# Gated delta rule in a hybrid layer: 32x32 diagonal blocks inverted by substitution on GpSimd, gates and key products moved ahead of the query and value convolutions

## The chip, the cores and the metric

The program runs on one core of a Trainium2 chip. The metric is device time in microseconds (us); several runs of a kernel are compared by their median. The engines are TensorE (PE; its weight loads are listed as PEld), VectorE (DVE), ScalarE (ACT), GpSimd (POOL) and SyncE (SP), which here issues nearly all DMAs.

## The reference, cut to what matters

One step of a hybrid layer, all in float32, for 512 prompt tokens and 64 sample tokens, with a model width of 1024. In the order of the computation: RMS norm and one input projection; a short convolution with SiLU over q, k and v; the gated delta rule with 4 heads of 128; differential attention; output projection; attention over a memory of 256 rows; a feed-forward block of 4096; a last norm. The change lies in the gated delta rule:

```
G    = cumsum(g)                                # per chunk of tokens
gam  = where(tril, exp(G[i] - G[j]), 0)
a    = where(strict, beta[i] * (k k^T) * gam, 0) + I
u, w = triangular_solve(a, [beta * v, beta * exp(G) * k])     # unit lower triangular
qk   = (q k^T) * gam
# scan over the chunks with the state S:
vn = u - w S;  o = (q exp(G)) S + qk vn;  S = S exp(G_last) + (k exp(G_last - G))^T vn
```

The norms of q and k are divided out along the way. The kernel takes chunks of 128 tokens (four of the prompt) and one of 64 (the sample), so that there are 18 heads-times-chunks groups of 32 rows: 4 chunks of 4 blocks and one of 2, each for 4 heads, 72 blocks of 32 by 32 in all.

## The kernel before, in words

Weights come in blocks of 128 columns by `weights`: a DMA into one of three buffers `raw`, a cast to `wh` on ACT (L164), the remainder `wl` on DVE (L165). `project` multiplies a block with the normed tokens on PE (L110), in a half of 256 tokens and one of 320, into three PSUM banks `pr`; a callback empties each bank (for the half of 256 a copy on ACT and an addition on DVE, L197 and L198). A scheduler fixes the order of the instructions on each engine when the program is built; an engine then works through its own list and waits on semaphores, so whatever stands behind a waiting instruction waits too.

Stages in order: 12 convolution blocks, k first, then q, then v (L407 to L427); the gates (L429 to L504), whose matmul takes the columns `wab`; the norm of the memory rows (L517 to L529); level masks `lev` (L533 to L549); for each chunk `gdn_prep`; the z projection, 4 blocks (`project_z`); `gdn_scan` for each chunk, beside which the projections of the differential attention run; the attention itself; and from `pr<-wh,u` on the keys and values of the memory and the rest of the layer.

`gdn_prep` builds the strict upper triangular `At` of a chunk for 4 heads (L617), and inverts I+At by doubling: from blocks of 1 (X and its transpose Dt) to 2, 4, 8, 16, 32 and 64. Each level takes a masked copy `B` of At on DVE (L642), a product with Dt and a copy `Y` on ACT (L664), a product with X, a subtraction from Dt on DVE (L669), and a transposition of Dt, copied to X on ACT (L673). The banks `g0` (even chunks) and `g1` (odd chunks) hold these products; `gs` holds those of the scan. `rpow` (L211) takes a power on GpSimd.

Of the kernel before, what the change touches and what calls it, by code (L numbers as in the profile page):

```python
# [34 lines left out]
def hybrid_layer_kernel(  # L35
# [373 lines left out]
    for typ in (1, 0, 2):
        cT[typ] = (e5[:, 1], e2[:, 1], e2[:, 0])[typ]  # L410
        for h in range(H):
            m = typ * 4 + h
            if m in FIRST:
                project(wts[m], xs, ev[m], halves=HALVES[1:])
            else:
                project(weights(w2, m * P), xs, conv_input(m))
            cb = cbs[m]
            G.tensor_copy(cb[:, SOFF : SOFF + 3], cwt[:, m, 4:7])
            n = SOFF + DEC
            yv = small("yv", [P, 584])  # L420
            A.activation(yv[:, :n], cb[:, :n], AF.Identity, scale=cwt[:, m, 0:1])  # L421
            for i in range(1, 4):
                V.scalar_tensor_tensor(yv[:, :n], cb[:, i : i + n], cwt[:, m, i : i + 1], yv[:, :n], ALU.mult, ALU.add)  # L423
            A.activation(cT[typ][:, h, :SEQ], yv[:, :SEQ], AF.Silu)
            A.activation(cT[typ][:, h, SEQ:], yv[:, SOFF:n], AF.Silu)
            G.tensor_copy(cst[:, m, 0:3], cb[:, SEQ : SEQ + 3])
            G.tensor_copy(cst[:, m, 3:6], cb[:, SOFF + DEC : SOFF + DEC + 3])  # L427

        if typ == 1:  # L429
            with tc.issue_after(opened[mybir.EngineType.PE]), tc.issue_after(opened[mybir.EngineType.Activation]):  # L430
                for q in range(2):
                    for t in range(0 if q else 2, 5):
                        raw_out(t, q, turn(xt[t], TT[t][1], q, f"g{t % 2}"))
            for i in range(2):
                nc.sync.dma_start(hd[i], hst[i])

# [68 lines left out]


# [8 lines left out]


    mt = view(e3, 0, 2, D)  # L517
    tc.keep_in_program_order(nc.sync.dma_start(mt, mem_prompt[0].rearrange("(b p) d -> p b d", p=P)))
    gkv = gain_rows(ln_mem_kv[0], "qz1")
    mn = view(e5, 0, 2, D)  # L520
    mhl = pair(4, F32R)
    mh, ml = view(mhl, 0, KT, NMEM), view(mhl, 1, KT, NMEM)
    for bi in range(2):
        scale(mn[:, bi, :], mt[:, bi, :], root(squares(mn[:, bi, :], mt[:, bi, :], P), P), gkv, P)
        for q in range(2):
            src = turn(mn[:, bi, :], P, q, "ba")
            mhi, mlo = (x[:, 4 * q : 4 * q + 4, bi * P : (bi + 1) * P] for x in (mh, ml))
            A.copy(mhi, src)
            V.tensor_tensor(mlo, src, mhi.bitcast(F32), ALU.subtract)  # L529


    with tc.issue_after(opened[mybir.EngineType.DVE]), tc.issue_after(opened[mybir.EngineType.Pool]):
        lev = const([P, P], "lev")  # L533
        prev = ident
        for lb in range(7):
            s = 2 << lb
            e = small("X", [P, P])
            G.memset(e, 1.0)
            ev = e.rearrange("p (n s) -> p n s", s=s)
            G.affine_select(out=ev, in_=ev, pattern=[[-s, P // s], [0, s]], compare_op=ALU.is_ge, fill=0.0, base=0, channel_multiplier=1)  # L540
            G.affine_select(out=ev, in_=ev, pattern=[[s, P // s], [0, s]], compare_op=ALU.is_ge, fill=0.0, base=s - 1, channel_multiplier=-1)
            m = small("B0", [P, P])
            V.tensor_tensor(m, e, prev, ALU.subtract)
            if lb == 0:
                V.tensor_copy(lev, m)
            else:
                V.scalar_tensor_tensor(lev, m, float(1 << lb), lev, ALU.mult, ALU.add)
            prev = e
        V.tensor_tensor(lev, lev, triu, ALU.mult)  # L549


    ck, cq, cv_ = cT[1], cT[0], cT[2]
    chunks = [(c, c * 128, c * 128, 128) for c in range(4)] + [(4, 512, 512, 64)]

    def v4(ap, n):
        return ap.rearrange("p (h n) -> p h n", h=4)[:, :, :n]

    def sb(tag, bufs=2):
        return small(tag, [P, 4, P], bufs)
# [654 lines left out]
```

## Time and profile before

| | |
|---|---|
| median of 3 runs | 1062.87 us (1062.4 to 1063.59) |
| span of the profiled execution | 1061.8 us |
| PE busy | 1037.3 us (98%) |
| DVE busy | 673.3 us (63%) |
| ACT busy | 433.7 us (41%) |
| POOL busy | 72.5 us (7%) |
| PE in the chain that ended last | 89% |

The profiled execution's own time is its span of 1061.8 us; the runs' median stands 1.1 us above it. The first matmul of the memory's keys, after which the change touches no order that matters for the delta rule, starts at 374.09 us. A reader looks first at the busy shares, then at the chain that ended last, then at the windows by stage, and at what PE waited for in the stage that changes.

### The profile page before, as it was taken

What the parts mean: (1) busy time and instruction counts of PE and PEld (TensorE: products, weight loads), DVE (VectorE), ACT (ScalarE), POOL (GpSimd) and SP (SyncE); (2) the same over time, 40 slices, a digit from 0 to 9 for tenths busy, and PEclk for the clock granted to TensorE, in tenths of its full rate; (3) what the DMA queues carried; (4) which work ended last, traced back from release to release, by engine and by line L of the source; (5) the groups of instructions that cost most, each with busy time, mean ns of one, the idle gap of its engine ahead of it and who ended that gap; (6) DMA issues with size and microseconds to landing.
All of it is one profiled execution on the core that took longest, in us unless ns stands there. A gap on an engine that the chain in (4) does not pass through costs nothing.

```text
span 1061.8 us, 16966 instructions
## 1 busy us (share of the span) xinstructions
PE 1037.3 (98%) x6574; PEld 933.5 (88%) x6574; DVE 673.3 (63%) x1487; ACT 433.7 (41%) x905; POOL 72.5 (7%) x126
## 2 busy tenths in 40 slices
PE   8999999999999999999999999999999999999997
PEld 6999889898788877999887799999999999999996
DVE  6766684766567575564554666666666666666774
ACT  6644754333265665343333443323232323222344
POOL 4311120221000000000000000000000000000000
PEclk9999999999999999999999999999999999999998
DMA  7332310100132255524111132232314141313312
GB/s 211 109 125 70 122 40 21 42 1 22 41 100 63 67 200 198 165 80 141 58 40 40 47 90 64 60 99 60 105 55 120 50 120 50 110 54 110 92 53 90
DMA packets 139443, 89.97 MB, mean 85 GB/s; under 512 B 5522, under 2 KB 130576, under 8 KB 138852
## 3 DMA queue, kind: packets, MB, share of 16 engines
q1 hardware_dynamic: 138996, 88.24, 27.9%
q8 instruction: 52, 0.85, 0.3%
q10 hardware_dynamic: 368, 0.66, 0.2%
q14 instruction: 27, 0.22, 0.1%
HBM read 79.14 MB, written 9.74 MB: 84 GB/s over the span
## 4 chain that ended last, share of the span: by engine, by line
PE 89%; issue 4%; DVE 3%; ACT 2%; POOL 1%; DMA 0%; POOLq 0%; ACTq 0%
PE pr L110 69%; PE g L110 9%; PE gs L110 3%; PE ba L116 3%; PE ba L110 2%; PE g L116 2%; POOL tg L211 1%; DVE B L642 0%; DMA out_dram<-p 0%; POOL tiny L211 0%; PE pr L116 0%; DVE wl L165 0%; DVE Dt L669 0%; PE gs L116 0%; ACT wh L164 0%
## 5 line engine op out<-in xcount | busy, mean ns | idle before, releaser
L110 PE MATMUL pr<-x,wh 128*128 128x512 f32 (+1 forms) x2664 | 700.2, 344 | 1.1 <-DVE u L953 0.6
L110 PEld LDWEIGHTS pr<-x,wh 128*128 128x128 f32 x2664 | 457.5, 189 | 36.9 <-issue 1.1
L110 PE MATMUL pr<-x,wl 128*128 128x256 f32 (+1 forms) x1776 | 486.3, 300 | 0.0
L110 PEld LDWEIGHTS pr<-x,wl 128*128 128x128 f32 x1776 | 329.4, 189 | 8.4 <-issue 0.4
L164 ACT CAST wh<-raw 128x1024 fp32r<-128x1024 f32 (+1 forms) x153 | 136.5, 892 | 232.8 <-PE pr L110 218.3
L165 DVE TENSOR_TENSOR wl<-raw,wh 128x1024 fp32r<-128x1024 f32 (+1 forms) x153 | 157.4, 1029 | 61.9 <-ACT wh L164 60.2
L953 DVE TENSOR_TENSOR u<-u,pr 128x256 f32<-128x256 f32 (+1 forms) x160 | 72.5, 453 | 63.4 <-PE pr L110 60.5
L211 POOL TENSOR_TENSOR tiny<-tiny,nhalf 128x1 f32<-128x1 f32 (+4 forms) x11 | 10.1, 916 | 665.8 <-DVE tiny L1144 409.2
L204 ACT CAST x<-p 128x256 fp32r<-128x256 f32 x64 | 27.8, 434 | 51.8 <-DVE p L1081 51.8
L110 PE MATMUL pr<-wh,u 128*128 128x512 f32 x128 | 41.4, 401 | 0.0
L205 DVE TENSOR_TENSOR x<-p,x 128x256 fp32r<-128x256 f32 x64 | 29.2, 457 | 15.1 <-ACT x L204 15.1
L197 ACT COPY p<-pr 128x256 f32<-128x256 f32 (+1 forms) x44 | 16.4, 373 | 51.5 <-PE pr L110 51.5
L198 DVE TENSOR_TENSOR p<-pr,p 128x256 f32<-128x256 f32 (+1 forms) x44 | 18.6, 423 | 26.6 <-ACT p L197 26.6
L955 DVE TENSOR_TENSOR u<-u,pr 128x256 f32<-128x256 f32 x80 | 33.6, 420 | 2.4
L1080 DVE TENSOR_TENSOR p<-pr,rB 128x320 f32<-128x320 f32 x32 | 15.7, 491 | 26.0 <-PE pr L110 26.0
L423 DVE SCALAR_TENSOR_TENSOR p<-p,gcol,p 128x579 f32<-128x579 f32 x33 | 27.1, 821 | 6.4 <-ACT p L421 5.9
L1081 DVE SCALAR_TENSOR_TENSOR p<-p 128x256 f32<-128x256 f32 x64 | 29.3, 458 | 2.2
L673 ACT COPY X<-g 128x512 f32<-128x512 f32 (+1 forms) x24 | 13.2, 550 | 42.6 <-PE g L116 42.5
L110 PE MATMUL g<-u,qz 128*128 128x256 f32 (+4 forms) x96 | 29.6, 409 | 0.1
L207 ACT ACTIVATE x<-u,gcol 128x256 fp32r<-128x256 f32 (+1 forms) x32 | 17.0, 534 | 30.7 <-DVE u L955 30.7
L642 DVE SCALAR_TENSOR_TENSOR B<-lev,At 128x512 f32<-128x512 f32 (+1 forms) x30 | 20.8, 697 | 10.6 <-PE g L110 8.8
L110 PEld LDWEIGHTS pr<-wh,u 128*128 128x128 f32 x128 | 23.3, 189 | 4.2
(319 smaller groups left out, 1217.7 us busy)
## 6 DMA issues: line engine op xcount, KB each, us to landing
raw<-in_w_ff_dram SPq DMA_DIRECT2D x32, 512.0 KB
raw<-in_w_ff_dram SPq DMA_DIRECT2D x64, 256.0 KB
raw<-in_w_in_dram SPq DMA_DIRECT2D x28, 512.0 KB
raw<-in_w_mem_k_dram SPq DMA_DIRECT2D x8, 512.0 KB
raw<-in_w_mem_v_dram SPq DMA_DIRECT2D x8, 512.0 KB
raw<-in_w_out_dram SPq DMA_DIRECT2D x8, 512.0 KB
raw<-in_w_mem_q_dram SPq DMA_DIRECT2D x8, 512.0 KB
raw<-in_w_mem_o_dram SPq DMA_DIRECT2D x8, 512.0 KB
```

The lines of the kernel that those rows point to most:

```text
L110: i = nc.tensor.matmul(out, lhsT, rhs, start=start, stop=stop)
L116: i = nc.tensor.transpose(out, in_, ident[:n, :n])
L164: A.copy(wh, raw)
L165: V.tensor_tensor(wl, raw, wh.bitcast(F32), ALU.subtract)
L204: A.copy(h, src)
L205: V.tensor_tensor(lo, src, h.bitcast(F32), ALU.subtract)
L211: G.tensor_tensor(out, in_, bc(nhalf[: in_.shape[0], 0:1], list(in_.shape)), ALU.pow)
L423: V.scalar_tensor_tensor(yv[:, :n], cb[:, i : i + n], cwt[:, m, i : i + 1], yv[:, :n], ALU.mult, ALU.add)
L642: V.scalar_tensor_tensor(B[:n, :, :n], lev[:n, :n].unsqueeze(1).to_broadcast([n, 4, n]), float(lv), At[:n, :, :n], ALU.is_equal, ALU.mult,)
L953: V.tensor_tensor(hm, hm, b, ALU.add)
L955: V.tensor_tensor(hm, hm, more, ALU.add)
L1081: V.scalar_tensor_tensor(f, f, 0.0, f, ALU.max, ALU.mult)
```

## The change

The doubling up to blocks of 32 goes. Of every `At` the 32x32 diagonal blocks of all chunks and heads are gathered, through DRAM (`dA`), on 72 partitions, one block to a partition, and inverted there together by forward substitution on GpSimd: 31 steps of a product (L586) and a subtraction (L590). The result goes through DRAM (`dD`) into the diagonal of each chunk's `Dt`; a transposition on DVE (L662) gives X, and the levels 32 and 64 follow as before.

For this the gates come after the first k block; `gr` holds the cumulated gates as rows, which go through DRAM (`dG`) and come back broadcast over the partitions (`g_rows`) in place of the matmul with `triu`. The decays `gam`, the products `k k^T` and `At` of all chunks are made once the k blocks are done, and then the q and v blocks follow. `gdn_prep` is parted into `gdn_products` and `gdn_inverse`; z is projected whole between the products of chunk 0 and its inverse. The norm of the memory rows moves behind the scans, with smaller loads; some buffers change places, and the memory's values are projected before its keys.

```diff
+    def conv_block(typ, h):
...
+    conv_block(1, 0)
...  (gates)
     mm(gsum[:, 0:20], triu, ggf)
     mm(gsum[:, 20:40], ones, ggf)
+    gr = bank()
+    mm(gr[:20, :P], ggf, triu)
+    grow_s = small("B1", [20, P])
+    A.copy(grow_s, gr[:20, :P])
+    nc.sync.dma_start(dG, grow_s)
...
+    for h in range(1, H):
+        conv_block(1, h)
...
+    def g_rows(c):
+        t = sb("B0" if c % 2 else "B1")
+        nc.sync.dma_start(t.rearrange("p h n -> p (h n)"), dG[4 * c : 4 * c + 4, :].rearrange("h i -> (h i)").partition_broadcast(P))
+        return t
...
+    for c, c0, t0, n in chunks:
+        g = g_rows(c)
+        for h in range(H):
+            V.scalar_tensor_tensor(
+                gam[c][:, h], g[:n, h, :n], Gc[:n, c, h : h + 1], cap[:n, :n], ALU.subtract, ALU.min
+            )
+    A.activation(gam4, gam4, AF.Exp)
+    A.activation(gam[4], gam[4], AF.Exp)
+    for c, c0, t0, n in chunks:
+        bkk = bank(f"g{c % 2}")
+        for h in range(H):
+            mm(bkk[:n, h * P : h * P + n], ck[:, h, L], ck[:, h, L])
+        dg = sb("Y" + str(c % 2))
+        V.tensor_tensor(dg[:n, :, :n], v4(bkk, n)[:n], ident[...], ALU.mult)
+        V.tensor_reduce(sk[:n, c, :], dg[:n, :, :n], AX.X, ALU.add)
...
+        for h in range(H):
+            V.scalar_tensor_tensor(
+                At[c][:, h], bkk[:n, h * P : h * P + n], brk[:n, c, h : h + 1], gam[c][:, h], ALU.mult, ALU.mult
+            )
+        nc.sync.dma_start(dA[c], At[c])
+        for b in range(n // BL):
+            nc.sync.dma_start(
+                AB[at : at + 4].rearrange("h (r i) -> h r i", r=BL), dA[c][bs, :, bs].rearrange("r h i -> h r i")
+            )
...
+    for j in range(BL - 1):
+        m, w = BL - 1 - j, j + 1
+        t = tmp[:, : m * w].rearrange("p (i c) -> p i c", c=w)
+        G.tensor_tensor(
+            t, U[:, j, w:].unsqueeze(2).to_broadcast([NB, m, w]), Di[:, j, :w].unsqueeze(1).to_broadcast([NB, m, w]),
+            ALU.mult,
+        )
+        G.tensor_tensor(Di[:, w:, :w], Di[:, w:, :w], t, ALU.subtract)
+    nc.sync.dma_start(dD, DB)
+
+    for typ in (0, 2):
+        for h in range(H):
+            conv_block(typ, h)
...
+    def gdn_inverse(c, n):
+        Dt, X, B = sb(f"Dt{c % 2}"), sb("X"), Bz[c % 2]
+        G.memset(Dt, 0.0)
+        for b in range(n // BL):
+            bs, at = slice(BL * b, BL * b + BL), 16 * c + 4 * b
+            nc.sync.dma_start(Dt[bs, :, bs], dD[at : at + 4].rearrange("h (r i) -> r h i", r=BL))
+        V.transpose(X.rearrange("p h n -> p (h n)"), Dt.rearrange("p h n -> p (h n)"))
+        for a in range(0, n, 2 * BL):
+            i, o = slice(a, a + BL), slice(a + BL, a + 2 * BL)
+            V.tensor_copy(B[i, :, o], At[c][i, :, o])
...  (the products of levels 32 and 64, as before)
     S = None
-    prepared = [gdn_prep(*chunks[0][:2], chunks[0][3])]
+    first = gdn_products(*chunks[0][:2], chunks[0][3])
+    project_z()
+    first["X"] = gdn_inverse(0, chunks[0][3])
+    prepared = [first]
     for c, c0, t0, n in chunks:
         if c < 4:
-            prepared.append(gdn_prep(*chunks[c + 1][:2], chunks[c + 1][3]))
+            prepared.append(prepare(c + 1))
...
-        if c == 0:
-            project_z()
         S = gdn_scan(c, c0, t0, n, prepared[c], S)
```

The built order moves instructions on GpSimd. Before, behind the last convolution block's small copies (`cst`), GpSimd's list goes on with the powers of the first two chunks' norms (`tg`, L211) and the masking of their decays (`Y`, L611):

```order
L426 COPY cst<-p_126_1011 128x3
L427 COPY cst<-p_126_1011 128x3
L211 TENSOR_TENSOR tg_1292<-tg_1293,nhalf 128x8
L211 TENSOR_TENSOR tg_1487<-tg_1488,nhalf 128x8
L611 TENSOR_TENSOR Y_176_1322<-Y_176_1322,triu 128x512
L611 TENSOR_TENSOR Y_226_1517<-Y_226_1517,triu 128x512
```

In the changed program the same place reads as follows. `nk` is the key norm, `tg_1421` the query norm of chunk 0, `tg_1707` that of chunk 1; `u_78` holds the blocks `AB` and `DB` from the first memset (L581) on.

```order
L581 MEMSET u_78 72x1024
L582 MEMSET u_78 72x32
L205 TENSOR_TENSOR nk<-sk,nhalf 128x20
L205 TENSOR_TENSOR tg_1421<-tg_1420,nhalf 128x4
L652 TENSOR_TENSOR u_75<-u_75,B_214_1742 128x4x128
L653 TENSOR_TENSOR u_78<-u_78,B_214_1742 128x4x128
L205 TENSOR_TENSOR tg_1707<-tg_1706,nhalf 128x4
L586 TENSOR_TENSOR u_78<-u_78 72x31
L590 TENSOR_TENSOR u_78<-u_78 72x31
L586 TENSOR_TENSOR u_78<-u_78 72x60
```

The 62 instructions of the substitution stand in one piece, behind the powers and the two products (L652, L653) of chunks 0 and 1.

On DVE the changed program's list at the end of the z projection is this. The rows on `pr` empty the 256-token halves of the four z blocks into `u_76` (the values end in 1462, 1514, 1566 and 1618); L159 makes the remainder `wl` of a weight block, the last one (`wl_2343`) of the first block of the differential attention; L662 transposes the `Dt` of chunks 0 and 1.

```order
L192 TENSOR_TENSOR u_76<-pr_1514,u_76 128x256
L159 TENSOR_TENSOR wl_1615<-raw_1612,wh_1614 128x1024
L662 STREAM_TRANSPOSE X_1665<-Dt_194_1664 128x512
L192 TENSOR_TENSOR u_76<-pr_1566,u_76 128x256
L662 STREAM_TRANSPOSE X_1748<-Dt_215_1747 128x512
L228 TENSOR_SCALAR tiny_2295<-tiny_2295 128x1
L1006 MEMSET tiny_4631 128x8
L192 TENSOR_TENSOR u_76<-pr_1618,u_76 128x256
L159 TENSOR_TENSOR wl_2343<-raw_2340,wh_2342 128x1024
```

Before, the z blocks' additions (L198) stood between the steps of the doubling, and no DVE instruction there took its input from a DMA except the remainders `wl`. Now the transposition of chunk 0, which does, stands ahead of the third z block's addition.

## Rows read from the trace of the kernel before

**Rows 1.** The page: busy time, and the chain of waits by engine.

```profile
PE 1037.3 (98%) x6574; PEld 933.5 (88%) x6574; DVE 673.3 (63%) x1487; ACT 433.7 (41%) x905; POOL 72.5 (7%) x126
...
PE 89%; issue 4%; DVE 3%; ACT 2%; POOL 1%; DMA 0%; POOLq 0%; ACTq 0%
```

**Rows 2.** Windows: stretch and length, busy time by engine, granted clock, DMA.

```profile
27.00:98.80 71.80, 71.80 (x466) 67.62 (x465) 48.35 (x86) 39.32 (x77) 17.51 (x58) 1.00 0.33 102
...
103.30:133.00 29.70, 27.26 (x185) 24.35 (x183) 21.43 (x73) 21.25 (x32) 4.54 (x3) 1.00 0.43 130
...
374.10:1061.80 687.70, 673.90 (x4092) 612.44 (x4090) 425.97 (x898) 244.56 (x483) 5.04 (x5) 0.99 0.30 90
```

**Rows 3.** What PE waited for, 103.3 to 374.1 us: total, times, longest.

```profile
PE g L110 <- DVE At L617: 2.1, 1, 2.1
...
PE g L110 <- ACT Y L664: 0.3, 1, 0.3
```

**Rows 4.** Groups of PE by form, 103 to 293 us: busy, mean ns.

```profile
L110 PE MATMUL g<-Y,X 128*128 128x128 f32 x160 | 22.9, 286 | 0.4 <-ACT Y L664 0.3
L110 PE MATMUL g<-Dt,B 128*128 128x128 f32 x160 | 22.1, 283 | 0.1
L116 PE MATMUL g<-ident,Dt 128*128 128x128 f32 x80 | 12.8, 281 | 0.0
L110 PE MATMUL g<-triu,gg 128*128 128x128 f32 x32 | 4.8, 284 | 0.0
```

**Rows 5.** PE in order of time: start, length, instruction.

```profile
98.81 4.34 PE L110 MATMUL pr<-x,wab 128*128 128x512 f32 x24
...
157.53 0.66 PE L116 MATMUL g<-ident,Dt 128*128 128x128 f32 x4
157.94 0.48 PE L110 MATMUL pr<-x,wh 128*128 128x512 f32 x1
...
165.25 2.05 PE L110 MATMUL g<-Y,X 128*128 128x128 f32 x16
167.13 0.60 PE L116 MATMUL g<-ident,Dt 128*128 128x128 f32 x4
```

**Rows 6.** Windows around PE's wait at 131 to 133 us.

```profile
134.00:138.30 4.30, 4.30 (x22) 3.87 (x21) 3.13 (x6) 3.32 (x6) 2.65 (x2) 0.60 0.45 121
```

**Rows 7.** Groups of POOL by form: busy, mean ns, idle before.

```profile
L637 POOL TENSOR_TENSOR u<-u,B 128x256 f32<-128x256 f32 x1 | 0.7, 726 | 3.8 <-PE g L110 3.8
L211 POOL TENSOR_TENSOR tg<-tg,nhalf 128x4 f32<-128x4 f32 x4 | 4.0, 1009 | 50.3 <-DVE tg L729 50.3
```

**Rows 8.** POOL in order of time.

```profile
20.30 2.89 POOL L540 TENSOR_SCALAR_AFFINE_SELECT X<-X 128x128 f32<-128x128 f32 x2
...
29.08 0.21 POOL L538 MEMSET X<- 128x128 f32 x1 [0.86 <-DVE B L543]
29.36 0.41 POOL L540 TENSOR_SCALAR_AFFINE_SELECT X<-X 128x128 f32<-128x128 f32 x1
...
149.83 1.28 POOL L637 TENSOR_TENSOR u<-u,B 128x512 f32<-128x512 f32 x1 [5.96 <-ACT Y L664]
151.07 1.74 POOL L638 TENSOR_TENSOR u<-u,B 128x512 f32<-128x512 f32 x1
```

**Rows 9.** What SP's queue waited for, 200 to 320 us.

```profile
SPq L747 <- DMA out_dram<-S: 1.8, 1, 1.8
```

**Rows 10.** SP in order of time.

```profile
291.90 0.38 SPq L751 DMA_DIRECT2D out_dram<-S  x1
```

**Rows 11.** Groups of DVE by form: busy, mean ns, idle before.

```profile
L165 DVE TENSOR_TENSOR wl<-raw,wh 128x1024 fp32r<-128x1024 f32 x97 | 118.8, 1225 | 54.8 <-ACT wh L164 53.2
L617 DVE SCALAR_TENSOR_TENSOR At<-g,tg,Y 128x128 f32<-128x128 f32 x16 | 4.6, 342 | 2.4 <-POOL Y L611 2.4
L633 DVE TENSOR_TENSOR vb<-g,tg 128x512 f32<-128x512 f32 x4 | 2.7, 684 | 0.1
```

**Rows 12.** ACT in order of time, the last v block.

```profile
106.27 0.63 ACT L424 ACTIVATE u<-p 128x512 f32<-128x512 f32 x1 [2.03 <-DVE p L423]
```

More of the change, by code (lines that the diff above doesn't have):

```diff
@@ L324, in conv_input @@
         cbs[m] = cb = small(tag, [P, 584])
-        G.memset(cb[:, 0:3], 0.0)
+        (G if m in FIRST else V).memset(cb[:, 0:3], 0.0)
         def evac(b, a0, n, more):
@@ L413, in hybrid_layer_kernel @@
             if m in FIRST:
-                project(wts[m], xs, ev[m], halves=HALVES[1:])
+                G.tensor_copy(cst[:, m, j : j + 3], cb[:, at : at + 3])
             else:
[L416 to L435, printed above, removed]
+                A.copy(cst[:, m, j : j + 3], cb[:, at : at + 3])
@@ L504, in hybrid_layer_kernel @@
     A.activation(kdc, kdc, AF.Exp)
+    for h in range(1, H):
+        conv_block(1, h)
+    with tc.issue_after(opened[mybir.EngineType.PE]), tc.issue_after(opened[mybir.EngineType.Activation]):
+        for q in range(2):
+            for t in range(0 if q else 2, 5):
+                raw_out(t, q, turn(xt[t], TT[t][1], q, f"g{t % 2}"))
+    for i in range(2):
+        nc.sync.dma_start(hd[i], hst[i])
+    BL = 32
+    chunks = [(c, c * 128, c * 128, 128) for c in range(4)] + [(4, 512, 512, 64)]
@@ new lines, in v4, with sb @@
+    def v4(ap, n):
+        return ap.rearrange("p (h n) -> p h n", h=4)[:, :, :n]
+    def sb(tag, bufs=2):
+        return small(tag, [P, 4, P], bufs)
+    with tc.issue_after(opened[mybir.EngineType.DVE]), tc.issue_after(opened[mybir.EngineType.Pool]):
+        cap = const([P, P], "cap")
+        G.memset(cap, 0.0)
+        G.affine_select(out=cap, in_=cap, pattern=[[1, P]], compare_op=ALU.is_ge, fill=-1e30, base=0, channel_multiplier=-1)
+        Bz = [sb(f"At{i}") for i in range(2)]
+        for z in Bz:
+            G.memset(z, 0.0)
@@ new lines, in hybrid_layer_kernel @@
+    gq = pair(4).rearrange("p a k t -> p (a k t)")
+    At4 = gq[:, :2048].rearrange("p (c h n) -> p c h n", c=4, h=4)
+    gam4 = gq[:, 2048:4096].rearrange("p (c h n) -> p c h n", c=4, h=4)
+    At = [At4[:, c] for c in range(4)] + [gq[:64, 4096:4352].rearrange("p (h n) -> p h n", h=4)]
+    gam = [gam4[:, c] for c in range(4)] + [gq[:64, 4352:].rearrange("p (h n) -> p h n", h=4)]
+    blk = e5[:, 0].rearrange("p k t -> p (k t)")
+    NB = 72
+    AB, DB, tmp = blk[:NB, :1024], blk[:NB, 1024:2048], blk[:NB, 2048:]
@@ new lines, in hybrid_layer_kernel @@
+    rpow(nk, sk)
+    V.tensor_tensor(nk, nk, sk, ALU.mult)
+    U, Di = (x.rearrange("p (r i) -> p r i", r=BL) for x in (AB, DB))
+    G.memset(DB, 0.0)
+    G.memset(DB[:, 0 : 1024 : BL + 1], 1.0)
+    for j in range(BL - 1):
[4 more added lines that the diff above has]
+            ALU.mult,
+        )
+        G.tensor_tensor(Di[:, w:, :w], Di[:, w:, :w], t, ALU.subtract)
@@ L514, in hybrid_layer_kernel @@
         nc.sync.dma_start(o_conv_s[0, 0][:, j * 512 : (j + 1) * 512], cso[3:6])
[L517 to L559, printed above, removed]
     zs = e3[:, 1]
@@ L689, in gdn_prep @@
-        return dict(kd=kd, vb=vb, X=X, KQ=KQ, brk=brk, rq=r8[:, 4:8], rq2=rq2)
+            tr(bt[:, h * P : h * P + n], Dt[:, h, :])
+        A.copy(X, v4(bt, n))
+        Y = sb(f"Y{c % 2}")
+        by = bank(f"g{c % 2}")
+        for h in range(H):
+            mm(by[64:, h * 64 : h * 64 + 64], At[c][:64, h, 64:], Dt[:64, h, :64])
+        A.copy(Y[64:, :, :64], by[64:, :256].rearrange("p (h n) -> p h n", h=4))
+        bx = bank(f"g{c % 2}")
+        for h in range(H):
+            mm(bx[:64, h * 64 : h * 64 + 64], Y[64:, h, :64], X[64:, h, 64:])
@@ L985, in norm_columns @@
         return r2
-    hx = [operand(i) for i in (4, 3)]
+    hx = [operand(i) for i in (4, 5)]
     for m in range(KT):
```

198 lines of the change are left out of this document (90 added, 108 removed).

## The prediction, made before the changed kernel ran

> **What bounds the kernel now.** First the page: PE is busy 98% of the span and is 89% of the chain that ended last, while GpSimd works 7% [rows 1]. Only work taken from PE, or a wait put onto it, moves the end. Then the windows by stage: the convolutions keep PE full until 98.8 us, with DVE busy 48.35 of 71.8 us beside it [rows 2]; the delta rule and what is interleaved with it run from 103.3 us to the first matmul on the memory at 374.1 us, 270.8 us; the 687.7 us behind that stay the same work [rows 2]. Last, PE's own waits in the middle stage: five groups from 2.1 down to 0.3 us, 5.7 us in all [rows 3]. After the longest the granted clock was 0.60 for 4.3 us [rows 6], between the two levels of 1.2 and 2.4 GHz, which cost 4.3 x 0.4 = 1.7 us. So the doubling, whose groups fill this stage [rows 4], is hardly waited for: it costs PE its matmul time. The built order keeps this so, since other matmuls stand between its steps.
>
> **What goes from PE.** Each of the two product forms has 160 records of 128x128 [rows 4], for 5 levels and 4 chunks; the level of 32 stays, so 4/5 go, 256, and with them the 32 of the decay rows `triu,gg`. Sixteen records start to start take 167.13 - 165.25 = 1.88 us [rows 5], 0.118 each: 288 x 0.118 = 34.0 us. Of the transpositions 80 go (the 80 of `ident,Dt` [rows 4] and 16 first ones, less 16 that stay), at 0.41 us for four (157.53 to 157.94 [rows 5]): 8.2 us. The chunk of 64, with smaller tiles and one level less, I estimate at 7 us, two thirds of a large chunk's 10.6. Sum 49 us. Each removed group also stood between matmuls of another kind; I take 4 us for these passages (bounds 0 and 8).
>
> **What the moved work costs on the way.** PE's list now has, ahead of the end of the last v block, the gates (4.34 us for `wab`, the same matmul as before [rows 5], and about 0.6 for the sums) and the key products of all chunks, 4 x 0.94 + 0.6 = 4.3 us. DVE gets there, for `gam` and `At`, 20 + 20 instructions like L617 at 0.342 us [rows 11], five masked products and five reductions near 0.684 us, and small ones near 0.2: 13.7 + 6.8 + 4 = about 25 us. Added to its 48.35 us this is 73 us of DVE work against 81 us of PE work, with chains through ACT and SP between. I no longer expect PE to be full: it comes early to the gate sums, to the fourth and fifth key product (whose banks `g0` and `g1` wait for the `At` before) and to one convolution bank. I take 12 us of waits (bounds 5 and 18). The last v matmul then ends at 98.8 + 4.3 + 0.6 + 4.3 + 12 = 120 us.
>
> **Where the substitution starts.** It needs only `At`, which I place near 92 us, and 23 small DMAs behind it at some 0.38 us of issue each [rows 10]: its input is there at about 103 us. But GpSimd works its list in order, and in front of the substitution stand the query-norm powers of chunks 0 and 1. The second waits on a DVE instruction that stands behind both `vb`, and these wait for the last v block. So: the last v block's SiLU came 106.9 - 98.8 = 8 us after the matmuls before [rows 12]; I take 6, since fewer casts lie beside it; then two groups of transpositions 0.9, on DVE `vb`, a reduction and `vb` at 0.684 each [rows 11] and a small one, the power at 1.0 [rows 7]: 120 + 6 + 0.9 + 2.3 + 1.0 = 130 us.
>
> **How long it takes.** 62 instructions with 2 x 5456 elements in a partition. A POOL product of 512 elements takes 1.28 us [rows 8], one of 256 0.726 [rows 7]: 2.16 ns an element and 0.17 us each, that is 23.6 + 10.7 = 34.3 us. Each waits for the one before; from a memset of 0.21 us to the select that needs it lie 0.28 us start to start [rows 8], 0.07 more: 62 x 0.07 = 4.3 us. The rest is what no row shows for this operation: 992 short inner rows, of 1 to 31 elements. Nearest are the selects. That with 16 rows of 8 took 0.41 us [rows 8] where a plain memset of as many elements took 0.21; 0.2/16 is 12 ns a row at most. The first two, of 64 rows of 2 and 32 of 4, took 2.89 us together [rows 8]: (2.89 - 2 x 0.21)/96 is 26 ns. Bounds 0 and 26 us; I take 8, nearer to the first, as the selects also compute an index and the 2.89 us lay beside busy DVE. Sum 47 us, bounds 35 and 65 (below the first only if GpSimd overlaps its instructions' fixed part, as 149.83 to 151.07 us might hint [rows 8]). It ends at 177 us.
>
> Beside DVE the product at 151.07 us took 1.74 us instead of 1.28 [rows 8]. The Trainium skill, "SBUF — State Buffer", section "Who interferes with whom", says that a DVE instruction with two SBUF inputs and a GpSimd instruction that reads SBUF exclude each other for a whole instruction; by that rule, three weight remainders of 1.225 us fall into the substitution and would put its end at up to 3.7 us later, some 181 us and a time near 1059 us. The row agrees in kind; I leave these microseconds in the range, since DVE stands still for most of that stretch.
>
> **Who waits for it.** `dD` goes to DRAM and comes back: an issue of 0.38 us [rows 10], 1.8 us until a reader of the result may start [rows 9], four reads of 0.38 and again 1.8: 5.5 us, so `Dt` of chunk 0 lands at about 182.6 us. On DVE the transposition that waits for it stands ahead of the third z block's addition (L192). PE meanwhile has only z: at 9,216 columns in 4.34 us [rows 5], a block of 13,824 takes 6.5 us. Three and a half blocks end some 22 us after z starts, at 152 to 155 us; the last half block lacks a bank and PE stands still for about 30 us (bounds 17 and 48). Behind the same DVE wait stands the remainder of the first attention projection, so nothing fills the gap. A lower clock afterwards costs about 2 us as above, and the inverses of chunks 0 and 1, now without filler between their steps, about 4.
>
> **The sum.** From `Dt`'s landing PE has, of the 270.8 us, what is left: less 5.7 + 1.7 of old waits and clock, 49 removed, 4 of passages, 22.4 of z that has gone before (4 x 6.5 less the last 3.6), 4.3 of key products, 4.5 of the products of chunks 0 and 1, 1.3 of the convolution state's transpositions: 177.9 us. The first memory matmul starts at 182.6 + 2 + 4 + 177.9 = 366.5 us instead of 374.1: 7.6 us earlier. The span of 1061.8 becomes 1054; from the runs' median, 1.1 us above it, **1055 us**. Per microsecond of substitution the end moves by one; at about 55 us nothing is gained. Early waits count the same way, through the v block, since the substitution waits for it.
>
> **The rivals.** *Substitution cheap*: no row cost, no dependence, 35 us or less. For it: large products stand back to back at 2.16 ns an element. Against it: 62 dependent instructions, most of them short. Then 12 us less, 1043 us. *Substitution dear, slower than before*: the short rows cost the selects' 26 ns, 992 x 0.026 = 26 us instead of 8, and the whole lasts 65 us; the point from which it decides is 55 us of substitution, and with 65 the time is 1055 + 18 = 1073 us. For it: the one row with really short rows; against it: the 12 ns row. *Early stage bound by DVE*: gate, decay and key work beside the k and q blocks makes PE wait 20 us instead of 12; 8 us more, 1063 us, no change. For it 73 us of DVE work with chains; against it that DVE stood idle for a third of that stretch. *The order does not bind*, the gap is covered by z: then 30 + 2 us more are gained, 1023 us. For it, that the input is there at 103 us; against it, the queue, which is fixed.
>
> **How the numbers follow.** Chances: the forecast 0.55, cheap 0.11, dear 0.25, DVE-bound 0.07, covered 0.02. About 0.2% (2 us) is what a measurement of this kernel can tell from no change. The forecast holds 0.52 of faster and 0.03 of same; with cheap and covered, faster is 0.65. Same: 0.03 and 0.04 from the DVE case, 0.07. Slower: 0.25 and 0.03, 0.28. The range runs from 1042, the cheap case, to 1073, the dear one; the forecast's own range is 1046 to 1062.
>
> **What would show it.** In the profile after: a block of L586 and L590 on POOL that starts only at about 130 us, behind the power of chunk 1, and lasts 47 us; one wait of PE of some 30 us from about 153 us on, put down to the addition at L192 or a DMA, with POOL busy all along; a few waits of 1 to 3 us between 50 and 125 us; PE's count of records smaller by about 450; the stretch from the first memory matmul to the end near 687.7 us. The prediction is wrong if POOL starts before 120 us, if its pace on short rows is far from 0.75 us an instruction, or if PE finds matmuls in the gap.

## The result, and the profile after

The changed kernel is slower, by about what the measurement can tell: 1065.47 us (median of 20 runs, 1060.29 to 1067.82) against 1062.63 us for the kernel before (20 runs, 1059.81 to 1064.71), a ratio of 1.0027 with an interval of 1.0016 to 1.0037. The forecast was 1055 us, faster.

The page of the changed kernel, beside [rows 1]:

```profile
PE 995.4 (94%) x6116; PEld 895.6 (84%) x6116; DVE 647.8 (61%) x1458; ACT 406.3 (38%) x869; POOL 85.7 (8%) x138
PE 69%; issue 2%; DVE 1%; ACT 1%; POOL 0%; POOLq 0%; ACTq 0%; DVEq 0%
```

PE has 458 records and 41.9 us of busy time less, while the span (1064.1 us) is 2.3 us longer: PE now stands still. The windows say where. The columns are those of [rows 2]: stretch, length, busy time of PE, PEld, DVE, ACT and POOL, granted clock, DMA. First the whole stage of the kernel before, up to its first memory matmul at 374.1:

```profile
26.00:374.10 348.10, 342.05 (x2396) 304.69 (x2394) 230.25 (x564) 173.06 (x392) 55.17 (x95) 1.00 0.22 64
```

The same stage of the changed kernel, to its first memory matmul at 376.4, then its parts and the rest:

```profile
26.00:376.40 350.40, 300.63 (x1928) 268.01 (x1926) 204.32 (x534) 145.43 (x356) 67.00 (x105) 0.92 0.27 75
26.00:83.00 57.00, 50.64 (x342) 46.85 (x341) 43.22 (x140) 35.78 (x67) 3.59 (x12) 0.99 0.51 152
83.00:98.00 15.00, 15.00 (x83) 13.79 (x82) 10.90 (x35) 6.38 (x18) 3.54 (x1) 0.81 0.29 82
98.00:133.80 35.80, 26.53 (x173) 23.43 (x171) 24.74 (x49) 14.11 (x34) 6.98 (x12) 0.94 0.08 18
133.80:139.60 5.80, 5.78 (x18) 4.72 (x19) 2.60 (x2) 1.04 (x1) 5.25 (x8) 0.50 1.09 277
156.00:173.20 17.20, 0.00 (x0) 0.00 (x0) 0.34 (x1) 2.76 (x5) 12.44 (x27) 0.62 0.06 17
173.20:177.40 4.20, 4.06 (x11) 3.17 (x12) 1.90 (x3) 0.46 (x2) 0.00 (x0) 0.51 0.20 31
183.70:189.30 5.60, 0.05 (x2) 0.01 (x1) 1.26 (x2) 2.34 (x5) 0.00 (x0) 0.85 0.37 94
189.30:193.00 3.70, 3.70 (x17) 3.70 (x18) 1.84 (x6) 0.42 (x1) 0.00 (x0) 0.50 0.55 139
193.00:300.00 107.00, 95.79 (x667) 85.36 (x666) 63.63 (x126) 28.17 (x56) 16.07 (x18) 0.93 0.24 61
376.40:1064.10 687.70, 673.97 (x4092) 612.09 (x4091) 426.33 (x898) 244.84 (x483) 5.04 (x5) 0.99 0.30 90
```

The last stretch is the 687.7 us of [rows 2] again. So all of the result lies in the stage ahead of it, and there it can be parted in three. Idle time is length less PE's busy time: 348.1 - 342.05 = 6.0 us before, 350.4 - 300.63 = 49.8 after. What a low clock costs is busy time times (1 - granted clock): summed over windows of 2 us, 1.7 before and about 17 after. The rest is work at full clock: 340.3 before and about 283 after. The change took 57 us of work from PE, and gave back 44 as waits and 15 as low clock: 2 us more in all.

The waits of PE in this stage, beside [rows 3] (total, times, longest):

```profile
PE pr L110 <- ACT u L615: 17.2, 1, 17.2
PE pr L110 <- ACT wh L158: 6.9, 2, 5.8
PE g L116 <- DVE KQ L643: 6.7, 3, 3.0
PE g L110 <- ACT Y L670: 5.6, 1, 5.6
PE g L110 <- DVE u L568: 4.3, 1, 4.3
```

Three of the five name ACT, an engine that works 38% of the span. Its list in order of time shows what it did ahead of the first and the fourth:

```profile
170.44 1.15 ACT L774 ACTIVATE raw<-raw,tiny 128x1024 f32<-128x1024 f32 x1 [22.91 <-POOL tiny L205]
171.49 0.40 ACT L615 ACTIVATE u<-u 128x256 f32<-128x256 f32 x1
171.80 1.03 ACT L158 CAST wh<-raw 128x1024 fp32r<-128x1024 f32 x1
...
182.25 1.15 ACT L774 ACTIVATE raw<-raw,tiny 128x1024 f32<-128x1024 f32 x1 [0.54 <-POOL tiny L205]
...
187.38 1.04 ACT L158 CAST wh<-raw 128x1024 fp32r<-128x1024 f32 x1 [2.82 <-DMA raw<-in_w_in_dram]
...
188.66 1.06 ACT L670 COPY Y<-g 128x512 f32<-128x512 f32 x2
```

L774 scales the first memory rows by their norm. It has nothing to do with the delta rule, but needs a power from GpSimd, and GpSimd is in the substitution:

```profile
124.28 1.01 POOL L205 TENSOR_TENSOR tg<-tg,nhalf 128x4 f32<-128x4 f32 x1 [34.27 <-DVE tg L634]
...
129.90 1.01 POOL L205 TENSOR_TENSOR tg<-tg,nhalf 128x4 f32<-128x4 f32 x1 [1.99 <-DVE tg L634]
130.87 0.23 POOL L586 TENSOR_TENSOR u<-u 72x31 f32<-72x31 f32 x1
...
133.57 0.42 POOL L590 TENSOR_TENSOR u<-u 72x112 f32<-72x112 f32 x1
...
151.10 0.62 POOL L586 TENSOR_TENSOR u<-u 72x256 f32<-72x256 f32 x1
...
167.27 0.42 POOL L590 TENSOR_TENSOR u<-u 72x112 f32<-72x112 f32 x1
...
169.63 0.25 POOL L590 TENSOR_TENSOR u<-u 72x31 f32<-72x31 f32 x1
169.84 0.56 POOL L205 TENSOR_TENSOR tiny<-tiny,nhalf 128x1 f32<-128x1 f32 x1
```

The power comes at 169.84, directly behind the last subtraction. On ACT the SiLU of z (L615) and the cast of the fourth z block's weights (L158) stand behind L774, so PE has no z from 156.0 to 173.2. The wait that the prediction had described stands close behind: on DVE the addition that empties a z bank (L192) came at 176.74, after the transposition of `Dt`. The built order of ACT shows the place (`raw_2266` are the memory rows, `wh_1614` the last z weights, `wh_2342` the first attention weights, `Y_197` the copy in the first inverse):

```
L774 ACTIVATE raw_2266<-raw_2265,tiny_2270 128x1024
L615 ACTIVATE u_76<-u_76 128x256
L158 CAST wh_1614<-raw_1612 128x1024
...
L158 CAST wh_2342<-raw_2340 128x1024
L615 ACTIVATE u_76<-pr_1638 128x320
L670 COPY Y_197_1679<-g_196_1674 128x512
```

`Y` is late by the memory norm too, through SP. The cast of `wh_2342` in front of it waits for a DMA that SP issues only at 183.42. On SP it stands behind the second load of memory rows (L772, 176.64), and the times say that it waits for more than its turn: ACT's scaling of these rows (L774) ends at 183.40, and rows and weights share the three buffers `raw`. In s_early the same two times are 162.62 and 162.65. So SP waits for a buffer that the norm holds.

```profile
169.91 0.32 SPq L591 DMA_DIRECT2D dD<-u  x1
172.88 3.66 SPq L661 DMA_DIRECT2D Dt<-dD  x8
176.64 0.38 SPq L772 DMA_DIRECT2D raw<-in_mem_prompt_dram  x1
183.42 6.67 SPq L154 DMA_DIRECT2D raw<-in_w_in_dram  x2
```

On DVE, the end of the hop through DRAM and, in its last rows, what stands ahead of one of the long waits for `KQ`:

```profile
176.10 0.71 DVE L662 STREAM_TRANSPOSE X<-Dt 128x512 f32<-128x512 f32 x1 [2.02 <-DMA Dt<-dD]
...
211.96 1.22 DVE L636 TENSOR_SCALAR tg<-tg 128x4 f32<-128x4 f32 x1 [1.12 <-POOL tg L205]
213.21 1.18 DVE L638 TENSOR_TENSOR tg<-tg 128x4 f32<-128x4 f32 x1
214.31 0.68 DVE L643 TENSOR_TENSOR KQ<-g,u 128x512 f32<-128x512 f32 x1
```

One group of PE by form, beside the 160 records of [rows 4]:

```profile
L110 PE MATMUL g<-Y,X 128*128 128x128 f32 x32 | 5.9, 354 | 5.6 <-ACT Y L670 5.6
```

The count is as worked out: a fifth is left (and 16 of the 80 transpositions of `Dt`).

### The profile page after: what moved, and what is told of

Its sections match the earlier page's. It is cut to its first block, busy times and chain, and to the rows that moved or that the text cites. A ratio compares the mean times of both kernels' runs of the same rounds, so it can differ in the third digit from the quotient of the medians.

```text
span 1064.1 us, 16001 instructions
## 1 busy us (share of the span) xinstructions
PE 995.4 (94%) x6116; PEld 895.6 (84%) x6116; DVE 647.8 (61%) x1458; ACT 406.3 (38%) x869; POOL 85.7 (8%) x138
## 4 chain that ended last, share of the span: by engine, by line
PE 69%; issue 2%; DVE 1%; ACT 1%; POOL 0%; POOLq 0%; ACTq 0%; DVEq 0%
PE pr L110 60%; PE g L110 4%; PE ba L110 2%; PE ba L116 2%; PE gs L110 1%; ACT u L1152 0%; POOL tiny L205 0%; POOL ta L205 0%; ACT p L1060 0%; ACT wh L158 0%; DVE u L979 0%; POOLq L1236 0%; DVE tiny L1057 0%; DVE an L913 0%; DVE p L1062 0%
## 5 line engine op out<-in xcount | busy, mean ns | idle before, releaser
L110 PE MATMUL pr<-x,wh 128*128 128x512 f32 (+1 forms) x2664 | 702.0, 345 | 27.2 <-ACT u L615 17.2
L158 ACT CAST wh<-raw 128x1024 fp32r<-128x1024 f32 (+1 forms) x153 | 136.4, 892 | 242.3 <-PE pr L110 217.4
L159 DVE TENSOR_TENSOR wl<-raw,wh 128x1024 fp32r<-128x1024 f32 (+1 forms) x153 | 158.0, 1033 | 89.5 <-ACT wh L158 87.4
L198 ACT CAST x<-p 128x256 fp32r<-128x256 f32 x64 | 27.8, 434 | 51.8 <-DVE p L1107 51.8
L191 ACT COPY p<-pr 128x256 f32<-128x256 f32 (+1 forms) x44 | 16.4, 372 | 50.5 <-PE pr L110 50.5
L192 DVE TENSOR_TENSOR p<-pr,p 128x256 f32<-128x256 f32 (+1 forms) x44 | 18.5, 421 | 24.8 <-ACT p L191 24.8
L110 PE MATMUL pr<-x,u 128*128 128x320 f32 (+2 forms) x160 | 26.5, 323 | 0.0
L116 PE MATMUL g<-ident,u 128*128 128x128 f32 (+2 forms) x116 | 18.2, 288 | 8.4 <-DVE KQ L643 6.7
```

Source lines behind the costliest of these rows:

```text
L110: i = nc.tensor.matmul(out, lhsT, rhs, start=start, stop=stop)
L116: i = nc.tensor.transpose(out, in_, ident[:n, :n])
L158: A.copy(wh, raw)
L159: V.tensor_tensor(wl, raw, wh.bitcast(F32), ALU.subtract)
L192: V.tensor_tensor(dst, b, dst, ALU.add)
L198: A.copy(h, src)
```

## The experiments

Three causes were in question: the substitution's late place on GpSimd's list, its length, and the memory norm whose power stands behind it. All times are medians, ratios are to the kernel before (1062.3 to 1062.8 us in these comparisons). "First" is the start of the first memory matmul in the profile, and the last column PE's busy time and granted clock in the 46.2 us from 133.8 to 180. Most kernels here ran four times, so a difference of 2 or 3 us between two of them is within their spread.

| kernel | median | ratio (interval) | first | PE, clock |
|---|---|---|---|---|
| changed kernel | 1065.47 | 1.0027 (1.0016 to 1.0037) | 376.5 | 28.84, 0.75 |
| s_nosub | 1043.75 | 0.9826 (0.9805 to 0.9848) | 353.6 | 39.07, 0.82 |
| s_early | 1044.04 | 0.9823 (0.9787 to 0.9859) | 357.4 | 40.16, 0.85 |
| s_mem | 1076.98 | 1.0140 (1.0113 to 1.0166) | 397.9 | 26.95, 0.76 |
| s_early_mem | 1057.04 | 0.9956 (0.9931 to 0.9981) | 379.5 | 43.67, 0.92 |
| s_mid | 1056.90 | 0.9949 (0.9933 to 0.9965) | 364.5 | 26.27, 0.76 |
| s_early_mid | 1036.44 | 0.9756 (0.9735 to 0.9777) | 345.4 | 45.07, 0.94 |
| s_half | 1054.50 | 0.9927 (0.9912 to 0.9942) | 364.9 | 34.71, 0.83 |
| s_nosub_late | 1040.60 | 0.9794 (0.9767 to 0.9820) | 353.2 | 29.78, 0.81 |
| s_z | 1060.69 | 0.9980 (0.9967 to 0.9993) | 371.6 | 27.74, 0.75 |
| s_early_mid_z | 1036.72 | 0.9766 (0.9749 to 0.9784) | 345.7 | 45.36, 0.94 |
| s_early_mid_qn | 1032.50 | 0.9710 (0.9686 to 0.9735) | 342.7 | 43.47, 0.92 |
| s_best | 1032.03 | 0.9709 (0.9689 to 0.9730) | 344.1 | 44.40, 0.93 |

**s_nosub: no substitution.**

```diff
-    for j in range(BL - 1):
+    for j in range(0):
```

> Leaves out the 62 products and subtractions on GpSimd (the inverse of each 32x32 block is then the identity); all else as in the changed kernel (1065.5 us). Theory A, the wait for the substitution is what ate the gain: z then runs through from 134 us, PE's wait of 17.2 us, the 5.6 us wait for Y and about 6 us of low clock behind them go, first memory matmul near 348 us, time 1034 to 1040 us. Rival B, the wait is only where slack of other engines shows (DVE and POOL work of the scans is late anyway): part of the time comes back as waits behind the scans, 1046 to 1056 us. Rival C, the early stage (gates, decays through DRAM) is the loss: 1058 us or more.

21.7 us less than the changed kernel: between the ranges of A and B, so neither holds as stated. Nor is it the clean price of the 39.0 us of substitution (130.87 to 169.88). Without them the scheduler planned another order: PE inverts chunks 0 and 1 and scans chunk 0 ahead of z, which starts at 155 us instead of 133.8.

**s_early: the products of each chunk, with their GpSimd powers, behind the substitution.**

```diff
         G.tensor_tensor(Di[:, w:, :w], Di[:, w:, :w], t, ALU.subtract)
+    sub_last = nc.cur_bb.bb.instructions[-1]
...
-    first = gdn_products(*chunks[0][:2], chunks[0][3])
+    with tc.issue_after(sub_last):
+        first = gdn_products(*chunks[0][:2], chunks[0][3])
```

(and the same around the call for the other chunks.)

> The same work, but GpSimd's query-norm powers and products of all chunks stand behind the substitution, so that it starts when its blocks are loaded, near 100 us instead of 131. Theory A: substitution done by 140 us, Dt lands near 147 us, before z is through: no gap, 1036 to 1046 us (some us lost where GpSimd and the convolutions' DVE instructions get in each other's way). Rival B: waits come back behind the scans, 1048 to 1058 us. Rival C: no more than 3 us faster than the changed kernel.

21.4 us less, as theory A has it, in runs that spread from 1038.37 to 1047.17. The order of PE's work is that of the changed kernel here. GpSimd in order of time, first and last instruction of the substitution:

```profile
102.15 0.23 POOL L586 TENSOR_TENSOR u<-u 72x31 f32<-72x31 f32 x1 [10.49 <-DMA u<-dA]
...
147.75 0.25 POOL L590 TENSOR_TENSOR u<-u 72x31 f32<-72x31 f32 x1
```

It starts when its data are there (the prediction had placed them at 103 us), takes 45.8 us beside the convolutions' work on DVE instead of 39.0, and still ends 22 us sooner. PE's wait of 17.2 us is gone: from 130 to 200 us its longest waits are 5.7 us for z's first weights, 3.7 for `Y` and 3.0 for `KQ`. So PE stood still for the late start of the substitution, 28.7 us behind two powers that do not concern it; with a start at 102 us its whole length is hidden.

**s_mem and s_early_mem: the memory norm (the loads L772, scaling L774 and transpositions of the memory rows) behind all four attention heads**, on the changed kernel and on s_early.

```diff
-    mhl = pair(4, F32R)
-    mh, ml = view(mhl, 0, KT, NMEM), view(mhl, 1, KT, NMEM)
-    for bi in range(2):
...
+    mhl = pair(4, F32R)
+    mh, ml = view(mhl, 0, KT, NMEM), view(mhl, 1, KT, NMEM)
+    for bi in range(2):
...
     ob = operand(3)
```

> Only the norm of the memory rows moves, behind the attention heads, so that neither ACT's scaling of them (which waits for a GpSimd power behind the substitution) nor their loads stand ahead of the last z block and of the first attention weights. The substitution stays late. Theory A with ACT's and SP's queues as second carriers of the wait: the fourth z block runs inside the gap (6.4 us) and the 5.6 us wait for Y goes: 1052 to 1057 us. Rival: only DVE's transposition carries the wait, then at most 3 us are gained, 1062 us or more.

> Both: early substitution and late memory norm. Theory A: with the gap gone the memory norm stands in nobody's way, so this is within 4 us of the early substitution alone, 1034 to 1044 us. Rival (queues matter by themselves): 6 us or more faster than the early substitution alone.

Both are slower than their base, by 11.5 and 13.0 us, which neither theory nor rival had. Windows of s_mem at the end of the attention:

```profile
340.00:380.00 40.00, 33.79 (x180) 26.66 (x178) 23.22 (x85) 22.40 (x77) 2.99 (x4) 0.87 0.37 122
380.00:397.80 17.80, 10.41 (x45) 7.09 (x44) 8.88 (x24) 8.86 (x29) 1.17 (x1) 0.74 0.00 0
```

PE is idle for 13.6 of 57.8 us there, while the changed kernel is full from 300 us to its first memory matmul (idle 0.01 us of 76.4). From 380.0 to 397.8 it is full too (17.80 us), with the memory matmuls among the last ones of the attention. They had filled the ends of the attention, and a norm that comes too late takes this filler away. The edit thus cost more than it brought, and says nothing yet on the norm's price in the gap.

**s_mid and s_early_mid: the same lines ahead of the third attention head.**

```diff
     for h in range(H):
+        if h == 2:
+            mhl = pair(4, F32R)
...
         diff_project(h)
```

> The changed kernel (1065.5 us) with the norm of the memory rows set ahead of the third attention head instead of ahead of the first (behind all heads it cost more at the end than it gave; the substitution stays late, behind the powers). Theory: the norm in the gap costs some 14 us by itself, as it holds ACT (last z block, 6.4 us), SP (first attention weights, 5.6 us of waiting for Y) and the clock behind both; the late memory matmuls stay fillers: 1050 to 1055 us. Rival: the norm was only an early user of idle time, no gain: 1062 us or more.

> Early substitution (1044.0 us alone) and the memory norm ahead of the third head. Theory: the two holds add, as up to the sample's chunk they did (19 and 14 us earlier alone, 32 together): 1028 to 1034 us. Rival, they are one wait: 1040 to 1044 us.

s_mid is 8.6 us faster than the changed kernel, s_early_mid 29.0: the two causes add up (21.4 + 8.6 = 30.0). Both times lie between theory and rival. And s_mid does not shorten the gap. Its matmul behind the gap:

```profile
177.23 0.90 PE L110 MATMUL pr<-x,wh 128*128 128x320 f32 x2 [19.78 <-DVE u L192]
```

This is the wait that the prediction had described, on the addition behind the transposition of `Dt`. The norm had only covered it, so ACT's hold of 22.9 us did not make PE's standstill longer. What goes is the wait of 5.6 us for `Y`, and low clock: the profiles have 49.8 us idle and 17 of clock in the changed kernel, 46.6 and 8.3 in s_mid. The profiled execution of s_mid is the fastest of ten (1053.99 us), so its size may flatter, but the kind is not an accident: the other pair has 31.9 idle and 14.8 of clock in s_early, 28.4 and 7.0 in s_early_mid, and all ten runs of s_mid show a mean granted clock of 0.976 to 0.979, the twenty of the changed kernel 0.969 to 0.975. So about 3 us of the norm's price are waits and the larger part is low clock. Why the clock holds when the norm comes later is not shown.

**s_half: 30 of the 31 subtractions left out**, so that the substitution is shorter and the rest of its order stands.

```diff
-        G.tensor_tensor(Di[:, w:, :w], Di[:, w:, :w], t, ALU.subtract)
+        if j == BL - 2:
+            G.tensor_tensor(Di[:, w:, :w], Di[:, w:, :w], t, ALU.subtract)
```

> Leaves out 30 of the 31 subtractions of the substitution (its inverse is then not the inverse); the products and all else as in the changed kernel (1065.5 us, substitution 39.0 us). The substitution shrinks to about 19 us and ends near 150 us instead of 169.9. Theory: the end follows the substitution one to one until the gap of 17.2 us is used up, so 17 to 20 us come off, as many as when all of it is left out (1043.8 us): 1044 to 1049 us. Rival: the end follows in proportion (21.7 us for 39), then 11 us, 1054 us or more.

11.0 us less than the changed kernel, the time of the rival. GpSimd's products last 20.10 us from 130.18. PE behind its gap:

```profile
158.47 0.90 PE L110 MATMUL pr<-x,wh 128*128 128x320 f32 x2 [6.78 <-DVE u L192]
```

With a substitution some 19 us shorter the gap shrinks by 10.4 us, and the end moves by 11. The scheduler planned another order for the shorter list (the load of memory rows now stands behind `dD` on SP), so the two numbers are not a clean slope, and the rival is not shown by them; what a microsecond less of substitution brings at an unchanged order stays open.

**s_nosub_late: no substitution, and all convolution blocks ahead of the gates again**, against s_nosub.

```diff
-    conv_block(1, 0)
+    for typ in (1, 0, 2):
+        for h in range(H):
+            conv_block(typ, h)
...
-    for h in range(1, H):
-        conv_block(1, h)
...
-    for typ in (0, 2):
-        for h in range(H):
-            conv_block(typ, h)
```

> Leaves out the 62 substitution instructions, as in the run of 1043.8 us, and has the gates, the decays and the key products behind all twelve convolution blocks, as before the change, instead of early. Theory: early placement costs PE about 10 us of waits and 3 us of clock there, but without it the decays' way through DRAM and the 23 gathers stand in the open behind the convolutions: same to 10 us slower, 1042 to 1055 us. Rival: the early placement is itself a main loss, then this is 6 us or more faster, 1038 us or less.

Only 3 us less than s_nosub, between theory and rival. Its windows:

```profile
26.00:133.80 107.80, 107.75 (x702) 100.29 (x702) 77.28 (x194) 68.46 (x135) 4.95 (x12) 1.00 0.40 117
133.80:180.00 46.20, 29.78 (x202) 25.65 (x200) 25.05 (x62) 13.09 (x21) 14.11 (x12) 0.81 0.18 45
```

PE is full to 133.8 us, and then idle for 16.4: the chains through gates, decays and DRAM take their time at either place. Without a substitution, placing them early costs no more than these 3 us; with one, no run tells.

**s_z, s_early_mid_z, s_early_mid_qn and s_best: two small moves.** In the first, the transpositions of the convolution state for the outputs come behind z:

```diff
-    for j in range(3):
-        b = bank()
-        for i in range(4):
-            tr(b[:6, i * P : (i + 1) * P], cst[:, 4 * j + i, :])
...
     prepared = [first]
+    for j in range(3):
+        b = bank()
+        for i in range(4):
+            tr(b[:6, i * P : (i + 1) * P], cst[:, 4 * j + i, :])
...
```

> The changed kernel with the outputs of the convolution state set behind the z projection, so that PE's wait of 5.8 us for z's first weights goes; the substitution stays late. Theory: z starts and ends 6 us earlier, the gap behind it grows by as much, the end is set by the substitution: same as the changed kernel within 3 us, 1062 to 1068 us. Rival: waits add up, then 6 to 9 us faster, 1057 to 1060 us.

> The same edit where no gap follows: early substitution, the norm of the memory ahead of the third head (1036.4 us) and z's weights free of the convolution state's outputs. Theory: here the 5.5 us of waiting and some 2 us of clock come off the end: 1028 to 1032 us, and the query-norm edit that the 1032.0 us kernel has besides is worth less than 3 us. Rival: nothing comes off, 1035 us or more.

s_z gains 4.8 us, between theory and rival, and s_early_mid_z nothing (+0.3), as its rival had it. In s_z too the built order changed: the second load of memory rows stands ahead of the reads of `Dt` and the first attention weights directly behind them, and the wait for `Y` falls from 5.55 to 2.77 us, while the gap stays.

```profile
173.14 0.80 PE L110 MATMUL pr<-x,wh 128*128 128x512 f32 x1 [17.06 <-ACT u L606]
...
186.59 2.65 PE L110 MATMUL g<-Y,X 128*128 128x128 f32 x16 [2.77 <-ACT Y L661]
```

SP issues these weights at 180.49, right behind the end of ACT's scaling at 180.46. That speaks again for the buffers that the norm holds as the cause of the wait for `Y`, but isn't a clean test of the edit.

In s_early_mid_z the edit does what it was meant to, and yet brings nothing. From 126 to 138 us PE waits 2.7 us instead of 6.7, but at the lower clock all along. A window of s_early_mid and the same one of s_early_mid_z:

```profile
130.00:132.00 2.00, 0.00 (x0) 0.00 (x0) 0.00 (x0) 0.00 (x0) 1.82 (x3) 0.50 0.99 259
130.00:132.00 2.00, 1.70 (x7) 1.58 (x7) 0.79 (x2) 0.00 (x0) 1.76 (x4) 0.50 0.00 0
```

Over the whole stage idle time falls from 28.4 to 24.9 us, and the cost of low clock rises from 7.0 to 11.4, of which 2.7 lie between 126 and 146 us.

In the second move, the query norm's scaling goes to the scan, so that `KQ` no longer stands behind it on DVE:

```diff
         rpow(r4[:n], s4[:n])
-        V.tensor_scalar(r4[:n], r4[:n], P ** -0.5, None, ALU.mult)
         rq2 = tiny([P, 4], "tg")
-        V.tensor_tensor(rq2[:n], r4[:n], r4[:n], ALU.mult)
...
     def gdn_scan(c, c0, t0, n, q, S):
         L = slice(c0, c0 + n)
+        V.tensor_scalar(q["rq"][:n], q["rq"][:n], P ** -0.5, None, ALU.mult)
+        V.tensor_tensor(q["rq2"][:n], q["rq"][:n], q["rq"][:n], ALU.mult)
```

> Early substitution, memory norm ahead of the third head, and the scaling of the query norms moved from the products into the scans, without the edit on the convolution state's outputs. Theory: of the 4.4 us between 1036.4 and 1032.0 us all belongs to the query norms, since in the scans DVE's two small instructions (some 1.2 us each beside GpSimd's products) no longer stand ahead of KQ, for which PE waited 3 us twice: 1030 to 1034 us. Rival: the two edits need each other: 1035 us or more.

> As the one before, and besides: the outputs of the convolution state behind the z projection, so that z's first weights don't queue behind them on SP (PE waited 5.7 us for that cast), and the scaling of the query norms moved into the scans, out of the way of KQ (two waits of 3 us). Theory: 5 to 12 us faster than early substitution with the norm ahead of the third head, 1018 to 1028 us. Rival: these waits are covered by others behind them, less than 3 us.

s_early_mid_qn is 3.9 us faster than s_early_mid, as its theory has it; the wait for `KQ` falls from 6.9 us in three (longest 3.0) to

```profile
PE g L116 <- DVE KQ L642: 4.4, 3, 1.7
```

These 2.5 us less of waiting are the larger part of the 3.9. s_best has both moves, misses its 1018 to 1028 us and is no faster than s_early_mid_qn (1032.03 and 1032.50): again idle time falls (25.7 to 21.6) and low clock rises (5.6 to 11.5). Either is 2.9% faster than the kernel before. So the change brings 30 of the 57 us that it takes from PE, once its order is right. The rest is still lost to waits and low clock, together 31 us in the profile of s_early_mid_qn against 8 before.

## Why the prediction was wrong

By the steps of the prediction:

- **Work taken from PE**: 49 + 4 forecast, 57 measured. Right within 4 us.
- **Early waits**: 12 us forecast up to the end of the last v block. It came at 119.8 us against 120, but with 7.5 us of waits and about 3.5 of low clock, which the term had not: right in its sum, partly by luck. Another 8.2 us of waits lie between there and z, 5.8 of them for z's first weights, which the prediction does not name. Up to 133.8 us it is 15.6 in all (57.00 - 50.64 + 35.80 - 26.53 and nothing from 83 to 98).
- **Start of the substitution**: 130 us forecast, behind the powers of chunks 0 and 1, 130.87 measured. Right, and s_early shows that this place is what PE stands still for.
- **Its length**: 47 us forecast, 39.0 measured. The mis-sized terms are the short rows, 8 us taken and nothing found: L590 with 112 elements takes 0.42 us at 133.57, as 28 rows of 4, and at 167.27, as 4 rows of 28. The price by element was near: 256 elements cost 0.62 (L586) where [rows 7] gave 0.726 for a product. Three weight remainders did fall into it, for which the prediction had left up to 3.7 us in its range: one GpSimd instruction beside each took some 0.9 us longer than usual (at 134.07, 135 elements in 1.28 us; at 165.80, 0.41), 2.6 us of the 39.0.
- **The hop**: 5.5 us forecast; from 169.88 to the transposition at 176.10 it took 6.2.
- **PE's standstill**: "about 30 us" forecast (the sum's own times make it some 34), 17.2 measured. It came at the place that was named, but was released by ACT, not by DVE's addition at L192, and a whole z block was still to do behind it and not half of one. It was shorter because the substitution ended 7 us sooner than forecast, because ACT released PE (173.2) before DVE would have (176.74), and because PE came to it some 8 us later than in the sum, after the waits ahead of z. None of the three was foreseen: for the time, it was luck.
- **Afterwards**: "The inverses of chunks 0 and 1 ... about 4" and "a lower clock afterwards costs about 2 us". Measured: 16.8 us of waits from 176 us to the first memory matmul, and 17 us of low clock over the stage, 10.6 of them behind the standstill. **These two terms are the failed steps.** Of the first, 5.6 us are `Y`, which stands on ACT behind a cast whose weights SP loads late, behind the memory rows and their scaling; 5.9 are two waits for `KQ`. Of the second, the windows show 2.9 us behind the wait of 5.8 (5.78 x 0.50), 2.0 behind the gap, 1.9 behind the wait for `Y`, 2.9 from 83 to 98, and 6.7 from 193 to 300.
- **The sum**: against the forecast's terms, work -4, waits up to z +4, standstill -17, waits behind it +13, clock +15: 11 us, where the first memory matmul came 10 us later than forecast (376.5 and 366.5).
- **"Per microsecond of substitution the end moves by one"**: open. In s_early, at the order of the changed kernel, the substitution ended 21.9 us sooner and the kernel 21.4 (18.7 between the two profiled executions). Leaving out all 39.0 us moved the end by 21.7 and about 19 us of it by 11, but both at another order.

The mechanism that the prediction did not price at all is the moved norm of the memory rows. The working followed the change through GpSimd's and DVE's lists, and not through ACT's and SP's, where an instruction of another stage now waits for GpSimd ahead of z, and a load and its buffers keep back the attention's weights. By s_mid the norm's place costs 8.6 us, more than the 7.6 that were forecast as a gain, of which the load explains some 3 to 6 us of waits; the low clock that goes with it stays unexplained. With the norm out of the gap the forecast's sign holds: 1056.90 us against 1055. That number is nearer than its parts, since the shorter substitution and the longer waits and lower clock behind it nearly cancel.

Of the rivals, "dear" gave the right sign for a wrong reason, as the short rows cost nothing; the cheap substitution (35 us or less) nearly came, at 39.0 us, and brought no gain; "the order does not bind" was wrong as s_early and s_early_mid show. "Early stage bound by DVE" (1063 us) had nearly the right time, but not by its mechanism: PE waited 7.5 us in that stage, fewer than the forecast's 12 and not 20.

## What to carry to other kernels

When a long piece of work goes onto an idle engine that works its list in order, list every instruction behind it on that engine and everyone who waits for those, on all queues, and of stages that have nothing to do with the change too; here a power of one element in each partition on GpSimd held ACT for 22.9 us, and the rows that it scales held the buffer of the next weights. Ask also what stands in front of it: 29 us of delay came from two powers that could as well follow. When a full engine is made to wait, count the low clock behind each wait beside the wait itself: here 15 us of clock came with 44 of waits. And when an experiment leaves work out, compare the order of the other work before the difference is called its price.
